# Two sums of weight blocks written over other tiles in a two-layer decoder on one core

## The chip, the core and the metric

The kernel runs on one core of a Trainium2 chip. Its time is the device time of one execution in microseconds (us). The engines are TensorE (PE), VectorE (DVE), ScalarE (ACT), GpSimd (POOL) and SyncE (SP); each runs its own instructions in the order in which they were put on its queue, and waits for the others by semaphores. SP issues the loads of the weights, POOL issues DMAs that add.

## The reference, cut to what matters

```python
def swiglu(h, w_gu, w_down):
    gate, up = jnp.split(h @ w_gu, 2, axis=-1)
    return (jax.nn.silu(gate) * up) @ w_down

def reference(x, mem, ...):
    for l in range(DEPTH):                      # 2 layers, x is 512 tokens x 1024
        x = x + 0.5 * swiglu(rmsnorm(x, g_ffn1[l]), w_ffn1_gu[l], w_ffn1_down[l])
        ...
        x = x + 0.5 * swiglu(rmsnorm(x, g_ffn2[l]), w_ffn2_gu[l], w_ffn2_down[l])
    return rmsnorm(x, g_final)
```

Between the two feed-forward networks (FFNs) of a layer stand a mixer (short convolution beside attention) and a cross-attention; the change does not touch them. All of it is in float32, and the inner width of an FFN is 2816.

## The kernel before, in words

**Precision.** A float32 product is made of three matmuls of a shorter type: each operand is split into a high part (hi) and the rest (lo), and hi times hi, hi times lo and lo times hi are added up. The split of the activations (here called the z split) is a cast on ACT (L644 for the down projection) and a subtraction on DVE (L645).

**Quads.** The FFNs use seven products in place of eight. A quad is four weight blocks 11, 12, 21 and 22; the seven products run in the order 1, 7, 6, 2, 5, 4, 3 (`ORDER`). Their weights are block 11 (product 1), T3 = 22 - 12 (product 7), T2 = T3 + 11 (product 6), block 21 (product 2), T1 = 12 - 11 (product 5), T4 = 21 - T2 (product 4) and block 22 (product 3). The sums T1 to T4 are made by `tt` (L83) on DVE. T3 is made in a tile of its own (`tmp`), T2 is written over T3 in the same tile, T1 over block 11 and T4 over block 21.

**Units.** Each product's weights come in two halves, a and b, called units here; T4a is the sum for the first half. A unit is one tile of 128x1024. `prefetch` splits a unit: the hi is a cast on ACT (L164, `whi<-big`). For the sums (products 7, 6, 5, 4) the lo is a subtraction on DVE (L169). For the raw blocks (products 1, 2, 3; marked "dma") ACT writes the negated hi (L166) and POOL issues a DMA that adds the raw block to it (L167, `wlo<-big`, "adding DMA" below). That DMA reads the raw block until it has landed, so whoever writes over the block waits for it. There are four buffers for units (`UNIT_BUFS`); a unit's hi can be written when PE has released the unit four before it.

**Order of work.** `ffn_plan` lists an FFN's work. An up-projection chunk is a quad of `w_gu` ("product"); a down-projection group is a quad of `w_down` over four or three rows of blocks ("group"). An FFN has three groups: in three of the four FFNs they begin at block 0, 6 and 14, in the last at 2 and 10 (two groups only). In a group the activations of a product are made ready one product ahead (`ready`: sums on DVE at L626, L630, L631, L637; then the z split), and each product is followed by updates of x on DVE (L670). The order on each engine's queue is then set by a scheduler from this program, with the tiles' dependences. Raw blocks come from twelve buffers (`BIG_BUFS`), each filled by a load on SP (L144, 512 KB) as soon as all that read or wrote its last content is done.

Of the kernel before, what the change touches and what calls it, by code (L numbers as in the profile page):

```python
# [8 lines left out]
ALU = mybir.AluOpType  # L9
# [32 lines left out]
class Weights:  # L42
# [30 lines left out]
    def quads(self, w, rows, cols, n):  # L73

        r, tmp = {}, {}
        parts = [(at, min(2, rows[0][1] - at)) for at in range(0, rows[0][1], 2)]

        def raw(q, h):
            at, nk = parts[h]
            r[q, h] = self.raw(w, rows[int(q[0]) - 1][0] + at, nk, (cols[int(q[1]) - 1], n))  # L80

        def tt(out, a, b, op):
            self.nc.vector.tensor_tensor(out=out, in0=a, in1=b, op=op)  # L83
            return out

        def block(q, h):
            return self.tiles[r[q, h]]

        def keep():
            pass  # L90

        def t3(h):
            tmp[h] = self.big((P, parts[h][1], n))
            return tt(tmp[h], block("22", h), block("12", h), ALU.subtract)

        def t2(h):
            return tt(tmp[h], tmp[h], block("11", h), ALU.add)

        def t1(h):
            return tt(block("11", h), block("12", h), block("11", h), ALU.subtract)  # L100

        def t4(h):
            return tt(block("21", h), block("21", h), tmp.pop(h), ALU.subtract)

        def freeing(*qs):
            return lambda: [self.free(r[q]) for q in qs]

        def product(i):
            for h in range(len(parts)):
                if i == 1:  # L110
                    raw("11", h)
                    self.unit(r["11", h], None, keep, "dma")
                elif i == 7:
                    raw("22", h)
                    raw("12", h)
                    self.unit(None, lambda h=h: t3(h), keep)
                elif i == 2:
                    raw("21", h)
                    self.unit(r["21", h], None, keep, "dma")
                elif i == 6:  # L120
                    self.unit(None, lambda h=h: t2(h), keep)
                elif i == 5:
                    self.unit(None, lambda h=h: t1(h), freeing(("11", h), ("12", h)))
                elif i == 4:
                    self.unit(None, lambda h=h: t4(h), freeing(("21", h)))
                else:
                    self.unit(r["22", h], None, freeing(("22", h)), "dma")

        return product
# [1227 lines left out]
```

## Time and profile before

| | us |
|---|---|
| median of 3 runs (2200.09 to 2204.6) | 2200.58 |
| profiled execution, own time | 2204.07 |
| its span in the profile | 2202.3 |
| PE busy in the span | 2134.5 (97%) |
| DVE busy | 1566.2 (71%) |
| ACT busy | 1357.5 (62%) |
| POOL busy | 258.4 (12%) |

The span runs from the first instruction to the last; 1.8 us of the execution's own time lie around it. A line such as `L83 DVE TENSOR_TENSOR big<-big` is an engine's operation at a line of the kernel with what it writes and reads; "idle before, releaser" is the time for which the engine stood idle just ahead of it, and what ended that.

### The profile page before, as it was taken

Reading aid. Unit: us, or ns where it says so; the run is one execution under the profiler, and the core shown is the slowest. Engines: PE = TensorE matmul, PEld = TensorE weight load, DVE = VectorE, ACT = ScalarE, POOL = GpSimd, SP = SyncE. Lnnn points to the kernel's source line nnn. Section 1 sums busy time; section 2 is a strip of 40 time slices with the busy share of each in tenths; the row PEclk is TensorE's granted clock in tenths of the full one; section 3 lists DMA queues with packets and bytes.
Section 4 is the critical chain, followed back from the end, with each engine's and each line's share of the span. In section 5 each row is a group of like instructions: output and inputs, shape, how many; then the busy total and the mean of one; then the engine's idle time right before and its main releaser. Section 6 shows DMA issues by size and latency. Waiting matters only on the chain. (4 is left out here: it accounts for less than half of the span.)

```text
span 2202.3 us, 30504 instructions
## 1 busy us (share of the span) xinstructions
PE 2134.5 (97%) x11602; PEld 1846.0 (84%) x11602; DVE 1566.2 (71%) x2196; ACT 1357.5 (62%) x1990; POOL 258.4 (12%) x293
## 2 busy tenths in 40 slices
PE   9999999999999999999999999999999999989998
PEld 7788889788888888888878888888888888778887
DVE  7677778778754768776777786777786557576775
ACT  7657566566443576667577666656664446556664
POOL 0111110122001011011001111101220010011110
PEclk9999999999999999999999999999999999999999
DMA  6776775223452367677646767642343422677672
GB/s 201 198 171 170 198 168 134 58 77 114 130 140 77 77 161 190 151 183 202 169 109 156 187 171 169 169 108 68 88 126 116 130 87 61 159 172 196 149 182 58
DMA packets 224185, 310.01 MB, mean 141 GB/s; under 512 B 12206, under 2 KB 128166, under 8 KB 224038
## 3 DMA queue, kind: packets, MB, share of 16 engines
q1 hardware_dynamic: 197222, 212.88, 31.7%
q0 software_dynamic: 26784, 95.17, 23.0%
q8 instruction: 91, 1.49, 0.3%
q14 instruction: 56, 0.46, 0.1%
q10 hardware_dynamic: 32, 0.01, 0.0%
HBM read 210.77 MB, written 2.10 MB: 97 GB/s over the span
## 5 line engine op out<-in xcount | busy, mean ns | idle before, releaser
L164 ACT CAST whi<-big 128x1024 fp32r<-128x1024 f32 x582 | 596.8, 1030 | 536.2 <-PE ps L216 227.6
L216 PE MATMUL ps<-whi,t 128*128 128x512 f32 x2624 | 817.1, 390 | 0.4 <-ACT t L220 0.2
L216 PEld LDWEIGHTS ps<-whi,t 128*128 128x128 f32 x2624 | 493.3, 188 | 102.6 <-ACT t L220 0.7
L169 DVE TENSOR_TENSOR wlo<-big,whi 128x1024 fp32r<-128x1024 f32 (+1 forms) x396 | 477.6, 1207 | 90.3 <-ACT whi L164 83.4
L216 PE MATMUL ps<-wlo,t 128*128 128x512 f32 x1312 | 513.3, 391 | 12.5 <-DMA wlo<-big 12.4
L216 PE MATMUL ps<-t,whi 128*128 128x512 f32 x1472 | 456.8, 391 | 1.5 <-ACT whi L855 1.5
L83 DVE TENSOR_TENSOR big<-big 128x1024 f32<-128x1024 f32 x248 | 294.3, 1196 | 219.0 <-DMA wlo<-big 212.6
L658 PE MATMUL ps<-t,whi 128*128 128x256 f32 x2296 | 427.6, 288 | 16.9 <-DVE t L645 15.8
L658 PEld LDWEIGHTS ps<-t,whi 128*128 128x128 f32 x2296 | 366.9, 196 | 21.2 <-DVE t L645 18.3
L658 PE MATMUL ps<-t,wlo 128*128 128x256 f32 x1148 | 330.6, 289 | 19.8 <-DMA wlo<-big 19.7
L216 PEld LDWEIGHTS ps<-t,whi 128*128 128x128 f32 x1472 | 274.5, 188 | 57.2 <-ACT whi L855 2.0
L167 POOL DMA_DIRECT2D wlo<-big x186 | 161.1, 866 | 1280.9 <-ACT wlo L166 732.0
L216 PEld LDWEIGHTS ps<-wlo,t 128*128 128x128 f32 x1312 | 246.7, 188 | 68.3 <-DMA wlo<-big 18.4
L216 PE MATMUL ps<-t,wlo 128*128 128x512 f32 x736 | 286.9, 390 | 1.1 <-DVE wlo L856 1.1
L658 PEld LDWEIGHTS ps<-t,wlo 128*128 128x128 f32 x1148 | 224.6, 196 | 24.2 <-DMA wlo<-big 24.1
L166 ACT ACTIVATE wlo<-big 128x1024 fp32r<-128x1024 f32 (+1 forms) x186 | 193.2, 1039 | 46.1 <-PE ps L216 45.3
L216 PEld LDWEIGHTS ps<-t,wlo 128*128 128x128 f32 x736 | 138.2, 188 | 30.7 <-DVE wlo L856 1.9
L670 DVE SCALAR_TENSOR_TENSOR x<-ps,x 128x512 f32<-128x512 f32 x154 | 102.7, 686 | 18.5 <-PE ps L658 18.3
L552 ACT COPY t<-ps 128x512 f32<-128x512 f32 x120 | 68.5, 586 | 31.2 <-PE ps L216 28.6
L926 POOL TENSOR_TENSOR t<-t,s 128x128 f32<-128x128 f32 (+1 forms) x64 | 60.2, 970 | 216.9 <-DVE s L924 182.3
L645 DVE TENSOR_TENSOR t<-t 128x512 fp32r<-128x512 f32 x88 | 57.0, 651 | 13.7 <-ACT t L644 13.6
L644 ACT CAST t<-t 128x512 fp32r<-128x512 f32 x88 | 50.6, 585 | 25.9 <-DVE t L631 16.4
(185 smaller groups left out, 1988.6 us busy)
## 6 DMA issues: line engine op xcount, KB each, us to landing
wlo<-big POOLq DMA_DIRECT2D x177, 512.0 KB, 5.4
big<-in_w_ffn_gu SPq DMA_DIRECT2D x160, 512.0 KB, 4.4
big<-in_w_ffn_down SPq DMA_DIRECT2D x80, 512.0 KB, 4.4
big<-in_w_mix_in SPq DMA_DIRECT2D x48, 512.0 KB, 3.9
big<-in_w_xkv SPq DMA_DIRECT2D x32, 512.0 KB, 4.0
big<-in_w_ffn_gu SPq DMA_DIRECT2D x32, 256.0 KB, 3.6
big<-in_w_mix_out SPq DMA_DIRECT2D x16, 512.0 KB, 4.6
big<-in_w_xq SPq DMA_DIRECT2D x16, 512.0 KB, 3.7
```

Of the source, the lines that this page charges most:

```text
L83: self.nc.vector.tensor_tensor(out=out, in0=a, in1=b, op=op)
L164: self.nc.scalar.copy(out=hi, in_=src)
L166: self.nc.scalar.activation(out=lo, in_=src, func=AF.Copy, scale=-1.0)
L167: self.nc.gpsimd.dma_start(out=lo, in_=src, accum_op=ALU.add)
L169: self.nc.vector.tensor_tensor(out=lo, in0=src, in1=hi.bitcast(F32), op=ALU.subtract)
L216: mm(ps, x, y, start=first and i == 0, stop=last and i == 2, skip_group_check=chained)
L552: nc.scalar.copy(out=s[i, e], in_=ps)
L644: nc.scalar.copy(out=hi, in_=o)
L645: nc.vector.tensor_tensor(out=lo, in0=o, in1=hi.bitcast(F32), op=ALU.subtract)
L658: mm(bank[f // 2][:, f % 2 * 256 : f % 2 * 256 + 256], w[y][:, k, f * P : (f + 1) * P], z[v][:, k, :], start=i in (1, 7, 2) and p == k == ...
L670: nc.vector.scalar_tensor_tensor(out=o, in0=bank[b].rearrange("p (f t) -> p f t", f=2), scalar=0.5, in1=o, op0=ALU.mult, op1=ALU.add,)
L926: nc.gpsimd.tensor_tensor(out=w[t], in0=w[t], in1=inv[:, t : t + 1].broadcast_to([P, (t + 1) * P]), op=ALU.mult)
```

## The change

```diff
         def t1(h):
-            return tt(block("11", h), block("12", h), block("11", h), ALU.subtract)
+            return tt(block("12", h), block("12", h), block("11", h), ALU.subtract)
 
         def t4(h):
-            return tt(block("21", h), block("21", h), tmp.pop(h), ALU.subtract)
+            return tt(tmp[h], block("21", h), tmp.pop(h), ALU.subtract)
```

T1 is now written over block 12, which no adding DMA reads, and T4 over the tile that holds T2. What the sums hold is the same. The scheduler puts them in other places of DVE's queue.

In the rows below the writes come left of the arrow. The place is the second FFN of layer 0, the group that begins at block 14; big_9360 and big_9381 are its blocks 11 (halves a and b), big_9586 and big_9613 blocks 12, big_9632 and big_9655 blocks 21, big_9771 and big_9793 the tiles of T3, T2 (and now T4). First DVE where the group's T3 is made. Before:

```order
L83 TENSOR_TENSOR big_9771<-big_9584,big_9586 128x1024
L83 TENSOR_TENSOR big_9793<-big_9611,big_9613 128x1024
L561 TENSOR_TENSOR t_9600<-ps_9522,t_9600 128x512
L561 TENSOR_TENSOR t_9602<-ps_9523,t_9602 128x512
L482 SCALAR_TENSOR_TENSOR t_9600<-t_9558,s_7151,t_9600 128x512
L482 SCALAR_TENSOR_TENSOR t_9602<-t_9560,s_7151,t_9602 128x512
L169 TENSOR_TENSOR wlo_9774<-big_9771,whi_9773 128x1024
L482 SCALAR_TENSOR_TENSOR t_9492<-ps_9455,s_7151,t_9492 128x512
```

With the change:

```order
L83 TENSOR_TENSOR big_9771<-big_9584,big_9586 128x1024
L83 TENSOR_TENSOR big_9586<-big_9586,big_9360 128x1024
L83 TENSOR_TENSOR big_9793<-big_9611,big_9613 128x1024
L561 TENSOR_TENSOR t_9600<-ps_9522,t_9600 128x512
L561 TENSOR_TENSOR t_9602<-ps_9523,t_9602 128x512
L83 TENSOR_TENSOR big_9613<-big_9613,big_9381 128x1024
L482 SCALAR_TENSOR_TENSOR t_9600<-t_9558,s_7151,t_9600 128x512
L482 SCALAR_TENSOR_TENSOR t_9602<-t_9560,s_7151,t_9602 128x512
L169 TENSOR_TENSOR wlo_9774<-big_9771,whi_9773 128x1024
```

T1a (`big_9586<-big_9586,big_9360`) stands between T3a and T3b, and T1b (`big_9613<-...`) before the L482; before, both came some ten rows later.

DVE in the same group at product 6, from its first `ready` sum (L630) on; t_9885 and t_9893 are the z splits of product 6, t_9959 and t_9963 those of product 2. Before:

```order
L630 TENSOR_TENSOR t_9881<-r_9501,r_9859 128x512
L83 TENSOR_TENSOR big_9360<-big_9586,big_9360 128x1024
L631 TENSOR_TENSOR t_9880<-t_9881,r_9501 128x512
L83 TENSOR_TENSOR big_9381<-big_9613,big_9381 128x1024
L670 SCALAR_TENSOR_TENSOR x2_156<-ps_9896,x2_156 128x2x256
L645 TENSOR_TENSOR t_9885<-t_9880,t_9884 128x512
L630 TENSOR_TENSOR t_9889<-r_9514,r_9872 128x512
L670 SCALAR_TENSOR_TENSOR x3_157<-ps_9897,x3_157 128x2x256
L631 TENSOR_TENSOR t_9888<-t_9889,r_9514 128x512
L645 TENSOR_TENSOR t_9893<-t_9888,t_9892 128x512
L83 TENSOR_TENSOR big_9632<-big_9632,big_9771 128x1024
L645 TENSOR_TENSOR t_9959<-r_9859,t_9958 128x512
```

With the change:

```order
L630 TENSOR_TENSOR t_9881<-r_9501,r_9859 128x512
L83 TENSOR_TENSOR big_9771<-big_9632,big_9771 128x1024
L631 TENSOR_TENSOR t_9880<-t_9881,r_9501 128x512
L83 TENSOR_TENSOR big_9793<-big_9655,big_9793 128x1024
L670 SCALAR_TENSOR_TENSOR x2_156<-ps_9896,x2_156 128x2x256
L645 TENSOR_TENSOR t_9885<-t_9880,t_9884 128x512
L630 TENSOR_TENSOR t_9889<-r_9514,r_9872 128x512
L670 SCALAR_TENSOR_TENSOR x3_157<-ps_9897,x3_157 128x2x256
L631 TENSOR_TENSOR t_9888<-t_9889,r_9514 128x512
L645 TENSOR_TENSOR t_9893<-t_9888,t_9892 128x512
L645 TENSOR_TENSOR t_9959<-r_9859,t_9958 128x512
```

T4a and T4b stand where T1a and T1b stood, and no L83 stands any more between the z splits of product 6 and of product 2.

DVE at the end of product 5 in the same group; wlo_10120 is the lo of unit 4b. Before:

```order
L670 SCALAR_TENSOR_TENSOR x0_154<-ps_10042,x0_154 128x2x256
L670 SCALAR_TENSOR_TENSOR x1_155<-ps_10043,x1_155 128x2x256
L645 TENSOR_TENSOR t_10111<-r_9859,t_10110 128x512
L83 TENSOR_TENSOR big_9655<-big_9655,big_9793 128x1024
L645 TENSOR_TENSOR t_10115<-r_9872,t_10114 128x512
L637 TENSOR_TENSOR t_10182<-r_9859,t_9880 128x512
L169 TENSOR_TENSOR wlo_10120<-big_9655,whi_10119 128x1024
```

With the change:

```order
L670 SCALAR_TENSOR_TENSOR x0_154<-ps_10042,x0_154 128x2x256
L645 TENSOR_TENSOR t_10111<-r_9859,t_10110 128x512
L670 SCALAR_TENSOR_TENSOR x1_155<-ps_10043,x1_155 128x2x256
L645 TENSOR_TENSOR t_10115<-r_9872,t_10114 128x512
L169 TENSOR_TENSOR wlo_10120<-big_9793,whi_10119 128x1024
```

T4b is gone from here, and the lo of 4b stands ahead of L637.

## Rows read from the trace of the kernel before

**Rows 1.** The page: the line of the quads' sums (busy, mean ns, idle before, releaser).
```profile
L83 DVE TENSOR_TENSOR big<-big 128x1024 f32<-128x1024 f32 x248 | 294.3, 1196 | 219.0 <-DMA wlo<-big 212.6
```

**Rows 2.** The list of waits, engine PE: us in total, times, longest.
```profile
PE ps L658 <- DMA wlo<-big: 19.7, 16, 2.6
PE ps L658 <- DVE t L645: 15.8, 11, 2.3
PE ps L216 <- DMA wlo<-big: 12.4, 13, 3.2
```

**Rows 3.** The list of waits, all engines, same columns: the sums, and ACT behind them.
```profile
DVE big L83 <- DMA wlo<-big: 212.6, 83, 6.7
...
ACT whi L164 <- DVE big L83: 114.4, 40, 5.5
```

**Rows 4.** The timeline of DVE, second FFN, group 14: start, us, engine, line.
```profile
1047.47 1.23 DVE L83 TENSOR_TENSOR big<-big 128x1024 f32<-128x1024 f32 x1 [1.30 <-DMA wlo<-big]
...
1050.09 1.42 DVE L482 SCALAR_TENSOR_TENSOR t<-t,s 128x512 f32<-128x512 f32 x2 [0.20 <-ACT t L479]
...
1061.57 1.22 DVE L83 TENSOR_TENSOR big<-big 128x1024 f32<-128x1024 f32 x1
...
1072.49 1.23 DVE L83 TENSOR_TENSOR big<-big 128x1024 f32<-128x1024 f32 x1 [3.59 <-DMA wlo<-big]
1073.64 0.69 DVE L645 TENSOR_TENSOR t<-r,t 128x512 fp32r<-128x512 f32 x1
```

**Rows 5.** The timeline of POOL, the same group: the adding DMA of block 21.
```profile
1065.30 0.86 POOL L167 DMA_DIRECT2D wlo<-big  x1 [17.84 <-DVE x L670]
```

**Rows 6.** The timeline of PE: matmuls that a z split released, at products 6 and 2.
```profile
939.18 0.38 PE L658 MATMUL ps<-t,whi 128*128 128x256 f32 x1 [1.30 <-DVE t L645]
...
947.19 0.58 PE L658 MATMUL ps<-t,whi 128*128 128x256 f32 x1 [1.92 <-DVE t L645]
...
1065.79 0.39 PE L658 MATMUL ps<-t,whi 128*128 128x256 f32 x1 [1.30 <-DVE t L645]
...
1074.38 0.39 PE L658 MATMUL ps<-t,whi 128*128 128x256 f32 x1 [1.10 <-DVE t L645]
...
2095.78 0.39 PE L658 MATMUL ps<-t,whi 128*128 128x256 f32 x1 [1.29 <-DVE t L645]
...
2103.49 0.38 PE L658 MATMUL ps<-t,whi 128*128 128x256 f32 x1 [1.64 <-DVE t L645]
```

**Rows 7.** The timelines of ACT and POOL, group 14: behind the second T4.
```profile
1083.77 2.00 ACT L164 CAST whi<-big 128x1024 fp32r<-128x1024 f32 x2 [4.32 <-DVE big L83]
...
1087.03 0.86 POOL L167 DMA_DIRECT2D wlo<-big  x1 [18.97 <-ACT wlo L166]
```

**Rows 8.** The timeline of PE: matmuls of product 3 that an adding DMA released.
```profile
239.29 0.39 PE L658 MATMUL ps<-t,wlo 128*128 128x256 f32 x1 [2.36 <-DMA wlo<-big]
...
880.66 0.38 PE L658 MATMUL ps<-t,wlo 128*128 128x256 f32 x1 [2.64 <-DMA wlo<-big]
...
1094.00 0.58 PE L658 MATMUL ps<-t,wlo 128*128 128x256 f32 x1 [1.97 <-DMA wlo<-big]
```

**Rows 9.** The timelines of SP, POOL and PE: the first product chunk of layer 1.
```profile
1139.20 0.37 SPq L144 DMA_DIRECT2D big<-in_w_ffn_gu  x1
...
1139.97 0.86 POOL L167 DMA_DIRECT2D wlo<-big  x1 [2.26 <-ACT wlo L166]
...
1147.91 0.50 PE L216 MATMUL ps<-wlo,t 128*128 128x512 f32 x1 [3.21 <-DMA wlo<-big]
```

**Rows 10.** Four stretches: PE, PEld, DVE, ACT, POOL busy, PEclk, DMA share, GB/s.
```profile
155.30:158.70 3.40, 3.40 (x18) 3.40 (x18) 1.22 (x1) 1.04 (x1) 0.00 (x0) 0.50 1.07 206
1066.70:1070.10 3.40, 3.40 (x18) 3.40 (x17) 1.52 (x3) 1.34 (x3) 0.86 (x1) 0.50 1.00 245
1238.50:1241.90 3.40, 3.40 (x29) 3.40 (x30) 2.42 (x3) 0.89 (x1) 0.86 (x1) 1.00 1.06 193
1978.00:1981.40 3.40, 3.40 (x19) 3.40 (x18) 3.40 (x6) 0.00 (x0) 0.00 (x0) 0.50 0.84 249
```

## The prediction

> **What bounds the kernel now.** PE is busy for 2134.5 us of a span of 2202.3 (the table above), so what a reordering can win lies in the 68 us in which PE stands idle, and in the stretches in which its clock is halved. I read the list of waits first, then the timelines around the places it names. DVE's sums wait 212.6 us for adding DMAs, 83 times [rows 3], which is nearly all the idle time in front of L83 [rows 1], and ACT's casts of units wait 114.4 us for those sums [rows 3]. That is a lot, and little of it reaches PE: PE waits 15.8 us for z splits, 19.7 us for adding DMAs in the groups and 12.4 us for them in the product chunks [rows 2]. 47.9 us is the ceiling; the sum below goes by these, not by the 212.6.
>
> How the two meet is seen in one group. T4a overwrites block 21, so it waits 3.59 us for the adding DMA that reads block 21 and was issued at 1065.30 [rows 4, 5]. The z split of product 2 (the L645 at 1073.64) stands behind it on DVE though it needs nothing of it, and PE idles 1.10 us until 1074.38 [rows 4, 6]. Ten us on, T4b is late in DVE's queue; the casts of units 4b and 3a on ACT wait 4.32 us for it, the adding DMA of 3a is issued at 1087.03 only, and PE stands for 1.97 us [rows 7, 8].
>
> **Part A: T4a no longer waits for an adding DMA.** The order shows T4a and T4b ahead of the z splits of product 6 and none behind. Of the 11 waits for a z split, five are at product 6 (first 939.18, last 2095.78, about 1.3 us each, 6.4 in all) and six at product 2 (first 947.19, last 2103.49), so these six hold 15.8 - 6.4 = 9.4 us [rows 2, 6]. What is late next is the landing itself: T4a could start at 1072.49 because the DMA had landed, and PE had come to product 2 at 1074.38 - 1.10 = 1073.28, 0.8 us later [rows 4, 6]. In the first group shown PE came at 945.27 [rows 6], about when T4a was released there. I take 0.4 us off for such places: **-9.0 us**; bounds -9.4 and 0 (the landing just takes the place of the split).
>
> **Part B: T1 moves ahead of product 6.** T1a now stands between T3a and T3b, where DVE waits 1.30 us for an adding DMA: it costs nothing, and if that wait were gone it would cost what T1b costs. T1b stands behind that wait, in front of L482, where the only cover is an idle 0.20 us [rows 4]. An L83 moves the next row back by 1.15 us (1072.49 to 1073.64), so everything behind it comes 0.95 us later, as T4a and T4b just fill the places that T1a and T1b held. Behind it stands the z split of product 6, for which PE waits in five groups already: 5 x 0.95 = 4.8 us. In a sixth (the first FFN's group at 6) one update of x comes ahead of that split as well, 1.15 + 0.6 us less what room there is; I take 1.5. In the other five groups T1b falls in idle time of DVE or ahead of work with room. **+6.3 us**; bounds 0 (the wait of T3 ends later or earlier than before and swallows it) and +8.
>
> **Part C: T4b is early, so 4b and 3a are cast on time.** Of the 16 waits for an adding DMA in groups, seven (first and largest 2.36 at 239.29, then 1.97 at 1094.00 among them) come of a late T4b: 7.4 us; two more, 1.2 us, are just behind the last group, among the 13 of the product chunks [rows 2, 8]. ACT's double cast at 1083.77 would go as soon as PE gives the buffers back; that is 1.6 us earlier for 3a, by my reading of where PE releases unit 5a, so of 1.97 us about 0.4 stay. Over all: **-7.6 us**. In the three first groups of an FFN (6.8 us, the largest 2.64 at 880.66 [rows 8]) I count nothing: the cast of 3a gains 0.5 us only before it meets its buffer's release, and two matmuls of the next chunk that filled that wait no longer stand in it. Bounds: 0 and -12.
>
> **Part D: loads go earlier.** Block 11 comes free when T2 has read it rather than when T1 is split. In the first chunk of layer 1, loads start at 1139.20, together with the adding DMA of unit 2b issued at 1139.97, which lands only just ahead of 1147.91 (7.9 us) and costs PE 3.21 us [rows 9]. With T2 releasing them the first two loads start some 8 us earlier, and are through when that DMA starts. Such first chunks hold 8.5 of the 12.4 us [rows 2]. I take 2.5 of the 3.21, 1.9 in the first chunk of the first FFN and 1.3 in the last FFN: **-5.7 us**; bounds 0 and -8.5.
>
> There the trace shows a slow adding DMA beside loads, and no more. The Trainium skill (DMA: Bandwidth & Descriptors, Queues, rings and completion order) says that each DMA engine goes round the queues that have work, packet by packet: loads and adding DMAs then share whatever time they overlap, and moving loads only moves the sharing. The trace agrees in so far as 7.9 us stand beside loads; by that rule part D is worth 0 if the loads meet another adding DMA, and the sum would be -14.5 in place of -20.2.
>
> **Clock.** Eight stretches of 3.4 us run at a granted clock of 0.50, the 1.2 GHz level (first 155.30, last 1978.00), each just behind gaps of PE; each loses 1.7 us. But a gap of 1.87 us ahead of 1238.50 was followed by a clock of 1.00, while product 6's gap of 1.30 was followed by 0.50 at 1066.70 [rows 6, 10]: the length of one gap does not decide. Five of the eight follow gaps that A, C and D take away. Product 6's longer gaps (2.2 us) may bring new ones; I take half of the places, 2.5. Net 2.5 x 1.7: **-4.2 us**; bounds -8.5 and +3.4.
>
> In the product chunks T4's waits of some 5 us cost PE nothing now, as the units there are made 2 to 5 us ahead, and I cost their end at nothing too; without that room each would show as a wait of PE at L216.
>
> **Sum:** -9.0 + 6.3 - 7.6 - 5.7 - 4.2 = -20.2 us against the profiled execution's own 2204.1 (its span and 1.8 us around it): 2183.9. That execution is 3.5 us above the median of the three runs, 2200.58; against the median the sum would be 2180.4. The profiled one may hold a halved stretch or two more than a usual run, so I stay near the upper: **2184**.
>
> **Rivals.** (1) **Product 6 becomes the bound and carries its delay on: slower.** T1b delays L644 and the ACT work behind it, so the adding DMA of 2a is issued later as well. If it takes over 0.8 us longer than PE is held up, the room between 1072.49 and 1073.28 is gone, its landing takes the place of T4a's wait and A is worth nothing. All six gaps at product 6 then halve the clock (6 - 4 stretches, +3.4), C and D give 2 each: 6.3 + 3.4 - 4 = +5.7, **2210**. For it: DVE has no idle time behind L482 there but 0.20 us. Against: PE is held up by the same 0.95, so the room stays. (2) **The clock falls at all the longer gaps** while the rest goes as forecast: -16 + 1.7 = -14, **2190**. For it 1066.70, against it 1238.50. (3) **The loads only meet other adding DMAs** and D is nothing: **2190**. For it, the 7.9 us beside loads; against it, in the order the loads wait for a landed DMA of block 11 or 21. (4) **Landings replace half of it**: A 4.5, C 2.5, D 2.5, clock nothing: -9.5 + 6.3 = -3.2, **2201**, no change. For it: 0.8 us is little room, and 3a's DMA took nearly 7 us (1087.03 to 1094.00). (5) **The change does not do what it says**: T4 would meet a new wait for the readers of T2's tile. The cast and the split of product 6 both stand ahead of it and are done by then, so this gets little; 2204.
>
> **Chances.** Forecast 0.55, (1) 0.06, (2) 0.17, (3) 0.10, (4) 0.10, (5) 0.02. What a measurement of this kernel can tell from no change is about 0.2%, 4.4 us. Faster: forecast, (2) and (3), 0.82. Same: (4) and (5), 0.12. Slower: (1), 0.06. The range starts where B is hidden by T3's wait and no new stretch is halved (-20.2 - 6.3 - 4.3 = -30.8, 2173; a little lower for the median) and ends at (4): 2172 to 2200.
>
> **What would show it.** In the profile after: DVE's waits at L83 for adding DMAs fall from 83 to about the 36 that belong to T3, some 90 us; PE's waits for z splits fall to five or six, each near 2.2 us, all at product 6, and none at product 2; the group of 19.7 falls to about 12; in the first chunk of layer 1 the adding DMA of 2b lands in under 6 us. Wrong would be a wait of PE for `wlo<-big` at product 2 as long as the split's was (rival 1 or 4), a wait of T4 for anything, or gaps at product 6 no longer than 1.3 us (B mis-sized).

## The result, and the profile after

The changed kernel takes 2174.94 us (median of 4, 2173.55 to 2176.87) against 2202.59 for the kernel before on the same chip (2200.09 to 2206.55): a ratio of 0.9873, 95% interval 0.9854 to 0.9892, 28 us faster. The profiled executions lie at 2176.87 and 2204.07, 27.2 us apart, and the accounts below go by these two.

The page of the changed kernel, to be held against the PE line of the table of before and [rows 1]:

```profile
PE 2124.5 (98%) x11602; PEld 1840.2 (85%) x11602; DVE 1568.4 (72%) x2196; ACT 1359.4 (62%) x1990; POOL 258.9 (12%) x293
...
L83 DVE TENSOR_TENSOR big<-big 128x1024 f32<-128x1024 f32 x248 | 294.0, 1196 | 61.1 <-DMA wlo<-big 58.0
```

The span is now 2175.1 us. PE stands idle for 50.6 us of it where it was 67.8, which is 17.2 us less. PE's busy time fell by 10.0 us with the same matmuls. DVE's idle time ahead of L83 fell from 219.0 to 61.1 us, and DVE is as busy as it was: the work stayed, and most of the waiting moved. DVE's idle time as a whole fell by 29 us only (from 636.1 to 606.7), since DVE now waits longer for ACT's casts ahead of the lo of a unit (L169). The list of waits for all engines, against [rows 3] (us in total, times, longest):

```profile
ACT whi L164 <- DVE big L83: 62.2, 20, 4.6
DVE big L83 <- DMA wlo<-big: 58.0, 29, 3.6
...
DVE wlo L169 <- ACT whi L164: 218.0, 190, 6.5
```

Before, the last of these was:

```profile
DVE wlo L169 <- ACT whi L164: 83.4, 130, 4.4
```

The waits of PE, the same columns, against [rows 2]:

```profile
PE ps L658 <- DMA wlo<-big: 11.5, 8, 2.6
PE ps L216 <- DMA wlo<-big: 10.2, 11, 2.1
PE ps L658 <- DVE t L645: 7.8, 6, 1.3
...
PE ps L658 <- ACT t L644: 2.2, 4, 0.9
```

Waits of PE for adding DMAs in the groups went from 19.7 to 11.5 us, those in the chunks from 12.4 to 10.2, those for z splits from 15.8 to 7.8; waits for a z cast (L644) rose from 0.7 to 2.2. These six at L645 are all at product 6; at product 2 there is none left.

DVE in the second FFN's group at 14, the group of [rows 4] (start, us, engine, line):

```profile
1042.89 3.74 DVE L83 TENSOR_TENSOR big<-big 128x1024 f32<-128x1024 f32 x3 [3.63 <-DMA wlo<-big]
...
1047.75 1.22 DVE L83 TENSOR_TENSOR big<-big 128x1024 f32<-128x1024 f32 x1
...
1060.13 1.22 DVE L83 TENSOR_TENSOR big<-big 128x1024 f32<-128x1024 f32 x1
...
1061.87 1.22 DVE L83 TENSOR_TENSOR big<-big 128x1024 f32<-128x1024 f32 x1
...
1063.60 0.69 DVE L645 TENSOR_TENSOR t<-t 128x512 fp32r<-128x512 f32 x1
...
1067.38 0.68 DVE L645 TENSOR_TENSOR t<-r,t 128x512 fp32r<-128x512 f32 x1
```

The first row holds T3a, T1a and T3b without a pause, where 1.30 us of waiting stood ahead of T3b. T1b (1047.75) follows, T4a and T4b (1060.13 and 1061.87) wait for nothing, and the z split of product 2 (1067.38) comes straight behind those of product 6. In [rows 4] it came at 1073.64.

PE at product 6, against [rows 6]; the first row is a group that had no gap before:

```profile
215.87 0.39 PE L658 MATMUL ps<-t,whi 128*128 128x256 f32 x1 [1.30 <-DVE t L645]
...
940.54 0.58 PE L658 MATMUL ps<-t,whi 128*128 128x256 f32 x1 [1.30 <-DVE t L645]
...
1062.66 0.39 PE L658 MATMUL ps<-t,whi 128*128 128x256 f32 x1 [0.53 <-ACT t L644]
...
1064.34 0.39 PE L658 MATMUL ps<-t,whi 128*128 128x256 f32 x1 [1.30 <-DVE t L645]
```

The wait for the low part (L645) is 1.30 us as it was; what grows is the wait for the cast ahead of it (0.53 here, where it was 0.30).

The first product chunk of layer 1, the rows of [rows 9]: POOL issues the adding DMA of unit 2b, PE's first matmul with it follows.

```profile
1132.40 0.86 POOL L167 DMA_DIRECT2D wlo<-big  x1 [2.26 <-ACT wlo L166]
...
1137.77 0.50 PE L216 MATMUL ps<-wlo,t 128*128 128x512 f32 x1 [0.90 <-DMA wlo<-big]
```

5.4 us from issue to use where it was 7.9, and a wait of 0.90 us where it was 3.21. The two loads that started 0.8 us ahead of this DMA and 1.0 us behind it now start 8.6 and 6.5 us ahead of it; two others start 1.5 and 2.9 us behind it. But the first chunk of layer 0's second FFN, which had no gap, now has one (POOL, SP, PE):

```profile
784.57 0.85 POOL L167 DMA_DIRECT2D wlo<-big  x1 [3.52 <-ACT wlo L166]
...
784.85 2.16 SPq L144 DMA_DIRECT2D big<-in_w_ffn_gu  x2
...
792.05 0.50 PE L216 MATMUL ps<-wlo,t 128*128 128x512 f32 x1 [2.13 <-DMA wlo<-big]
```

Here two loads start 0.3 and 2.1 us behind the adding DMA of 2b, which takes 7.4 us. In the kernel before, the same two started 1.9 and 3.0 us behind it, and it took 4.9 us. The list of DMA queues (packets, MB, share of the 16 DMA engines) shows what it waits for. From 785.5 to 788.0 only the loads' queue moves bytes:

```profile
q1 hardware_dynamic: 157, 0.32, 78.5%
```

The bytes of the adding DMA follow when the first load is through. In the first chunk of layer 1 it is the other way round: from 1132.4 to 1136.7 only POOL's queue moves bytes, though two loads are issued in that time. So in these places the transfers take turns as wholes, and what counts is whether a load goes out ahead of the adding DMA or just behind it.

The granted clock (columns as in [rows 10]): four stretches at 0.50 (first 155.40, last 2070.30) where there were eight; behind the gap of 1064.34 there is none.

```profile
155.40:158.80 3.40, 3.40 (x18) 3.40 (x18) 2.73 (x3) 0.88 (x1) 0.00 (x0) 0.50 1.03 195
216.90:220.30 3.40, 3.40 (x18) 3.40 (x17) 2.01 (x4) 1.34 (x4) 0.87 (x1) 0.50 1.05 198
940.50:943.90 3.40, 3.36 (x15) 3.36 (x16) 2.72 (x5) 2.29 (x4) 1.29 (x2) 0.50 0.81 153
1064.40:1067.80 3.40, 3.40 (x28) 3.40 (x29) 2.71 (x5) 2.72 (x5) 1.18 (x2) 1.00 0.82 154
2070.30:2073.70 3.40, 3.40 (x19) 3.40 (x18) 2.31 (x4) 1.53 (x3) 0.86 (x1) 0.50 0.99 187
```

### The profile page after: what moved, and what is told of

Read it like the earlier page. It is cut to its first block, busy times and chain, and to the rows that moved or that the text cites. A ratio compares the mean times of both kernels' runs of the same rounds, so it can differ in the third digit from the quotient of the medians.

```text
span 2175.1 us, 30582 instructions
## 1 busy us (share of the span) xinstructions
PE 2124.5 (98%) x11602; PEld 1840.2 (85%) x11602; DVE 1568.4 (72%) x2196; ACT 1359.4 (62%) x1990; POOL 258.9 (12%) x293
## 5 line engine op out<-in xcount | busy, mean ns | idle before, releaser
L169 DVE TENSOR_TENSOR wlo<-big,whi 128x1024 fp32r<-128x1024 f32 (+1 forms) x396 | 478.1, 1207 | 222.1 <-ACT whi L164 218.0
L216 PE MATMUL ps<-wlo,t 128*128 128x512 f32 x1312 | 512.4, 391 | 10.5 <-DMA wlo<-big 10.2
L658 PE MATMUL ps<-t,wlo 128*128 128x256 f32 x1148 | 327.6, 286 | 11.5 <-DMA wlo<-big 11.5
L83 DVE TENSOR_TENSOR big<-big 128x1024 f32<-128x1024 f32 x248 | 294.0, 1196 | 61.1 <-DMA wlo<-big 58.0
L926 POOL TENSOR_TENSOR t<-t,s 128x128 f32<-128x128 f32 (+1 forms) x64 | 60.2, 970 | 216.9 <-DVE s L924 182.2
L645 DVE TENSOR_TENSOR t<-t 128x512 fp32r<-128x512 f32 x88 | 57.0, 650 | 15.4 <-ACT t L644 15.1
L644 ACT CAST t<-t 128x512 fp32r<-128x512 f32 x88 | 51.1, 584 | 23.3 <-DVE t L631 15.3
```

Of the source, the lines that this page charges most:

```text
L169: self.nc.vector.tensor_tensor(out=lo, in0=src, in1=hi.bitcast(F32), op=ALU.subtract)
L216: mm(ps, x, y, start=first and i == 0, stop=last and i == 2, skip_group_check=chained)
L644: nc.scalar.copy(out=hi, in_=o)
L645: nc.vector.tensor_tensor(out=lo, in0=o, in1=hi.bitcast(F32), op=ALU.subtract)
L658: mm(bank[f // 2][:, f % 2 * 256 : f % 2 * 256 + 256], w[y][:, k, f * P : (f + 1) * P], z[v][:, k, :], start=i in (1, 7, 2) and p == k == ...
L926: nc.gpsimd.tensor_tensor(out=w[t], in0=w[t], in1=inv[:, t : t + 1].broadcast_to([P, (t + 1) * P]), op=ALU.mult)
```

## The experiments

All were timed beside the kernel before on the same chip. In the text, "product 6" stands for the waits of PE for z splits and casts there.

**Each half of the change alone.** T4 over T2's tile alone, then T1 over block 12 alone:

```diff
-            return tt(block("21", h), block("21", h), tmp.pop(h), ALU.subtract)
+            return tt(tmp[h], block("21", h), tmp.pop(h), ALU.subtract)
```
```diff
-            return tt(block("11", h), block("12", h), block("11", h), ALU.subtract)
+            return tt(block("12", h), block("12", h), block("11", h), ALU.subtract)
```

> Only T4 goes over T2's tile; T1 stays on block 11. Theory: T4's wait for an adding DMA, with the z splits and casts behind it, is the cost, so the six waits of PE for z splits at product 2 (9.4 us) and the seven for product 3 (7.4 us) go, with some half-clock stretches (4 to 8 us); but in DVE's order T1a, T1b and T4a now all stand ahead of the first z split of product 6, 1.15 us more than before, so the gaps at product 6 grow by 5 x 1.15 + 1.5 = 7 us. About 2188 beside 2202.6 for the kernel before, slower than the full change. Rival (T1's move brings the gain): within 4 us of the kernel before, waits at product 2 still there.

> Only T1 goes over block 12; T4 stays on block 21 and still waits for the adding DMA. Theory: what counts is what stands behind T4's wait. In the order both z splits of product 2 now stand ahead of T4a, so the six waits at product 2 (9.4 us) go without T4 having lost its wait (DVE keeps about 47 waits of T4); T1a and T1b no longer stand between L630 and the z split of product 6, whose gaps shrink from 1.3 to 1.5 us to under 1; T4b stays late, so the seven waits at product 3 (7.4 us) stay. About 2185. Rival (T4's wait itself has to go): no more than 4 us faster than the kernel before.

T4 alone: 2180.38 us, ratio 0.9907 (0.9891 to 0.9924). T1 alone: 2186.64, ratio 0.9923 (0.9905 to 0.9941). PE's waits with T4 alone:

```profile
PE ps L216 <- DMA wlo<-big: 12.9, 11, 2.1
PE ps L658 <- DVE t L645: 12.4, 10, 1.8
PE ps L658 <- DMA wlo<-big: 11.3, 8, 2.4
```

The six gaps at product 2 and the seven at product 3 are gone, as expected; the ten waits for z splits are all at product 6, 12.4 us where the full change has 7.8 and 2.2. So with T1 late three sums stand ahead of the first split there and T4b ahead of the second, and moving T1 out of that place is worth something by itself. The forecast of this run (2188) was 8 us too slow: the gaps at product 6 were sized about right (they grew by 5.4 us in all, to 12.4, where 7 had been expected), and what gave more is PE's busy time, 11.2 us less, with a mean granted clock of 0.996 where it was 0.993.

T1 alone: waits of DVE, then of PE.

```profile
DVE big L83 <- DMA wlo<-big: 189.1, 74, 6.0
```

```profile
PE ps L658 <- DMA wlo<-big: 23.2, 17, 2.6
```

DVE waits 189 us for adding DMAs where it was 212.6, and PE's waits for z splits fall to 1.0 us (three of 0.3, all at product 6), since in this order the splits of product 2 stand ahead of T4a. So what costs is what stands behind a wait; the wait of T4 by itself costs little. The waits at product 3 that were expected to stay fell as well, from 7.4 to 2.3 us. But the adding DMAs in the groups cost 23.2 us, more than before. One of them (POOL, then PE):

```profile
1067.64 0.86 POOL L167 DMA_DIRECT2D wlo<-big  x1 [2.89 <-ACT wlo L166]
...
1073.64 0.39 PE L658 MATMUL ps<-t,wlo 128*128 128x256 f32 x1 [2.06 <-DMA wlo<-big]
```

This is unit 2b. PE comes to product 2 earlier because product 6 holds it up no longer, and the DMA also goes out later: in this order three casts of activations (L644) stand on ACT just ahead of 2b's negated hi, and POOL issues at 1067.64 what it issues at 1065.75 in the changed kernel. That is the first rival's "landing takes the place of the split", without longer gaps at product 6; in the six groups it costs 8.6 us here. That the time forecast for this run (2185) came out is luck in part: these 8.6 us were not in it, and some 5 us of the waits at product 3 went that were to stay.

**What stands ahead of product 6's split.** The sums u + v of both halves are issued ahead of the differences:

```diff
+            for p, nk in pairs(c) if i == 6 else ():
+                u, v = (rows[(c, e), p][:, :nk, 256:] for e in "uv")
+                sums[c, 5, p] = T(shape=(P, 2, 256))[:, :nk, :]
+                nc.vector.tensor_add(out=sums[c, 5, p], in0=u, in1=v)
             for p, nk in pairs(c):
...
                     elif i == 6:
-                        v = rows[(c, "v"), p][:, :nk, :]
-                        sums[c, 5, p] = T(shape=(P, 2, 256))[:, :nk, :]
-                        nc.vector.tensor_add(out=sums[c, 5, p], in0=u[:, :, 256:], in1=v[:, :, 256:])
```

> The changed kernel again, on the chip of the three runs that follow: about 2175, with waits for z splits at product 6 of some 10 us.

> The changed kernel, and at product 6 of a group the sums u + v of both halves come first and the differences behind them, so that in DVE's order only one T4 and no update of x stands ahead of the first z split of product 6. Theory (what stands ahead of that split sets the gaps at product 6): the split comes 1.15 us earlier, and the 10 us at product 6 fall to 4 to 6; about 2170. Rival (the gaps at product 6 only cover late landings of product 2's adding DMAs): the waits for z splits fall as much and the waits for adding DMAs in the groups grow by as much; 2175.

The change again took 2173.27 us (ratio 0.9864, 0.9843 to 0.9885), the version with the sums first 2167.89 (0.9840, 0.9819 to 0.9861). Waits of PE, first the change again, then the sums first (its lines 645 and 658 are 646 and 659):

```profile
PE ps L216 <- DMA wlo<-big: 11.0, 13, 2.1
PE ps L658 <- DMA wlo<-big: 9.1, 8, 1.6
PE ps L658 <- DVE t L645: 7.8, 6, 1.3
...
PE ps L658 <- ACT t L644: 1.7, 3, 0.8
```

```profile
PE ps L216 <- DMA wlo<-big: 11.2, 13, 2.2
PE ps L659 <- DMA wlo<-big: 11.2, 11, 2.3
PE ps L659 <- DVE t L646: 2.8, 5, 0.7
```

Product 6 falls from 9.5 to 2.8 us. The adding DMAs in the groups grow by 2.1; new waits at product 2 hold 1.1 us. So the theory holds, with a small share for the rival: of 6.7 us won at one place some 2 come back at the next, and the median moved by 5.4. The intervals of this pair overlap (0.9843 to 0.9885 and 0.9819 to 0.9861); the same step is seen once more, and larger, in the last pair of runs below.

**Unit 2b of the first chunks.** Its lo is made on DVE in place of the adding DMA:

```diff
-                    self.unit(r["21", h], None, keep, "dma")
+                    self.unit(r["21", h], None, keep, False if first and h else "dma")
```

(`first` is true for the quads of chunk 1.)

> The changed kernel, and in the first product chunk of each FFN the lo of unit 2b is made by a subtraction on DVE and not by an adding DMA (four units). Theory: the 6.1 us that PE waits there for that DMA in the changed kernel (2.05, 2.13, 0.90, 1.04) come of its sharing the DMA engines with loads that were freed earlier, and they go, with a half-clock stretch or two: 2166 to 2170 beside about 2175 for the changed kernel. Rival (the unit is late for another reason, its casts or its buffer): PE waits there as long for DVE's lo, and the time stays at 2175.

> The change with the first chunks' unit 2b split on DVE, again, on one chip with the run that follows. With the sums first it was worth 8.6 us (2167.9 to 2159.3), on the change alone 1.3 at most. If the first measurement held a bad draw of landings, 2165 to 2168 now; if the gain needs the gaps at product 6 gone (their half-clock stretches and the later adding DMAs take it back), 2172 to 2175 again, with five or so half-clock stretches.

2173.69 us (ratio 0.9878, 0.9859 to 0.9896) and again 2172.25 (0.9844, 0.9816 to 0.9871). The two ratios lie on either side of the change's own (0.9873 and 0.9864), so by itself this is worth something between nothing and the 5 us that were expected, and the runs don't settle it. The gaps themselves did go. PE's waits in the second of these runs:

```profile
PE ps L658 <- DVE t L645: 7.8, 6, 1.3
PE ps L216 <- DMA wlo<-big: 5.8, 8, 2.3
```

In the chunks 5.8 us stay of 10.2 to 11.0 (8.2 in the first of the two, where later units wait more); at unit 2b of the first chunks no wait is left in either. That much of the theory holds: without that adding DMA there is no gap. The granted clock, 0.996 and 0.997 in the changed kernel's two profiles, was 0.996 and 0.995 in these, so no halved stretch went with the gaps; product 6's gaps are still there (7.8 us at L645).

**A pool of its own for T3.** T3 waits because its tile is the buffer that block 22 has just left. Given two buffers of its own (the pool of activations gives up four of 47), it waits for no adding DMA:

```diff
-T_BUFS = 47
+T_BUFS = 43
...
-            tmp[h] = self.big((P, parts[h][1], n))
+            tmp[h] = self.tmp_pool.tile(
+                [P, parts[h][1], n], F32, name="tmp", tag="tmp", padded_shape=[P, 1024 // n, n]
+            )
...
+    tmp_pool = ctx.enter_context(tc.tile_pool(name="tmp", bufs=2))
```

> The changed kernel, and T3 gets a pool of its own with two buffers in place of one of the twelve that hold blocks (the pool of activations gives up four of 47), so T3 no longer waits for the adding DMA of the chunk before. Theory (T3's wait at the head of a group makes product 6's split late, T1b only lengthens it): the 29 waits of 58 us at L83 go, and so do the 10 us at product 6; 2163 to 2168. Rival (T1 and T4 ahead of the split are the cause): the waits at product 6 stay at 6 us or more; 2173 or more. A third (two loads more run ahead, beside adding DMAs): waits for adding DMAs grow by what the splits give.

> The two runs before together: no gap at product 6 is left. If landings do not take their place, 2160 to 2166; if product 2's adding DMAs do (as with T1 alone moved), 2170 to 2175.

2205.48 us (ratio 1.0018, 1.0003 to 1.0032), and with the sums first as well 2203.49 (1.0004, 0.9992 to 1.0015): all that the change had won is lost. T3's waits for adding DMAs are gone and so is every wait at product 6, as the theory said; but the adding DMAs cost 52.5 us in place of 21.7 (lines 219 and 661 are 216 and 658 of the kernel before):

```profile
PE ps L219 <- DMA wlo<-big: 34.9, 31, 3.5
PE ps L661 <- DMA wlo<-big: 17.6, 18, 2.7
```

Some 40 us of it are at product 1, in chunks and groups, where the changed kernel waits 5.9 us. The waits account for some 21 us of the 29 between the two profiles (30.8 more at adding DMAs, 10.0 less at product 6); PE is also busy for 8.2 us more at the same mean clock, 0.996, and why is open. Two readings were left: two more blocks loaded ahead, or the loads' new places in time. The next run takes the two blocks away again:

```diff
-BIG_BUFS = 12
+BIG_BUFS = 10
...
-                W.limit = BIG_BUFS - 4
+                W.limit = BIG_BUFS - 2
...
-            W.limit = BIG_BUFS - 2
+            W.limit = BIG_BUFS
```

(on top of the first of these two runs, so without the sums first, and with `T_BUFS` at 47).

> As the run with a pool of two for T3, but blocks have ten buffers in place of twelve, so no load goes further ahead than in the changed kernel (and activations have their 47 again). Theory (in the run before, two more loads at a time ran beside product 1's adding DMAs, which landed after 7.5 to 9.4 us where 5 is usual): the waits of PE at product 1, 35 us there, fall below 10, T3 still waits for nothing and product 6 has no gap: 2162 to 2168. Rival (T3's wait kept DVE and ACT from other work that now comes ahead of product 1's): the waits at product 1 stay, 2195 to 2205.

2203.68 us (ratio 1.0006, 0.9991 to 1.0021): my theory of the two extra blocks fell, and so did the shortage of activations as a cause. What is left is when the loads go out, not how many are ahead. SP, POOL and PE in this run, at the second chunk of the first FFN:

```profile
74.52 3.56 SPq L146 DMA_DIRECT2D big<-in_w_ffn_down  x2
...
75.38 0.87 POOL L169 DMA_DIRECT2D wlo<-big  x1 [1.84 <-ACT wlo L168]
78.09 0.87 POOL L169 DMA_DIRECT2D wlo<-big  x1 [1.85 <-ACT wlo L168]
...
86.53 0.50 PE L219 MATMUL ps<-wlo,t 128*128 128x512 f32 x1 [1.06 <-DMA wlo<-big]
```

The row of SP holds two loads, the second of them at 77.74. They go out as soon as block 22's buffers are free, and beside them stand the two adding DMAs of product 1 (75.38 and 78.09), the second of which is used 8.4 us after its issue. In the changed kernel T3 takes these two buffers, no load goes out between 70.25 and 87.67, and the same two DMAs (issued at 77.16 and 79.88) land in 5.3 and 6.0 us. So T3's hold on these buffers, with the wait that looked like pure loss on DVE, keeps loads off product 1's DMAs. It is so all over the kernel: of the 186 adding DMAs, 10 in the changed kernel have a load that was issued less than 1 us ahead or 0.5 us behind, and 48 in this run; these land after 7.6 and 8.0 us on average, the others after 5.1 and 5.0.

The rival on record for this run, other work on DVE and ACT ahead of product 1's, had 2195 to 2205, where the time fell, but the rows speak against it. The adding DMAs that PE waits for here are issued as far ahead of PE as in the changed kernel (6.5 us on average, 6.3 there); they land 1.9 us later (7.6 and 5.7). A run that holds back these loads alone was not made.

**The two that helped, together.** Sums first, and the first chunks' 2b on DVE:

> Sums first at product 6, and the first chunks' unit 2b split on DVE, on top of the change: the two gains lie in different places (groups and first chunks), so if they add up 2164 to 2167; if what the first chunks give is taken back by later adding DMAs, as it was without the sums first, 2167 to 2169.

> The fastest version again (sums first, first chunks' 2b on DVE): 2158 to 2161, at most two half-clock stretches.

2159.33 us (ratio 0.9802, 0.9778 to 0.9825), and again 2161.52 (0.9795, 0.9775 to 0.9814): faster than both kernels, and by 5 us more than the first forecast, for which the two gains just add up. PE's waits in the first of them:

```profile
PE ps L659 <- DMA wlo<-big: 10.8, 9, 2.3
PE ps L216 <- DMA wlo<-big: 6.3, 8, 1.6
PE ps L659 <- DVE t L646: 3.2, 5, 0.7
```

The mean granted clock is 0.999 and 0.998. On one chip the second of them stands 10.7 us below the change with 2b alone (2172.25): some 6 us are product 6's gaps (10.4 to 4.1 in the two profiles), and (0.998 - 0.995) x 2160 = 6.5 us the clock: one stretch at 0.50 in place of five. But the clock's share is not product 6's alone. Of the four that are gone, two stood behind product 6's gaps (at 936.8 and 2063.2) and two behind landings of adding DMAs (875.3 and 2100.7, behind waits of 1.83 and 2.32 us). Why a given gap is followed by a halved stretch and another is not, stays open.

## Why the prediction was right, and where its sizes were off

The forecast was 2184 with a range of 2172 to 2200, and faster with 0.82; measured 2174.94. The sum was -20.2 us against the profiled execution; it came to -27.2. The direction and the mechanism held: T4 no longer waits, the splits and casts behind it are in time, and gaps and stretches at half clock go. That the number came within 10 us is luck in part: B's cost was set 3.3 us too high and D's gain 4.1 us too large, the clock's gain 2.6 us too small, and 5 us were in no term. By steps:

- **Part A (-9.0): right, with help that was not in it.** All six gaps at product 2 are gone, 9.4 us. The feared landing behind them did not show, for two reasons. PE is held up at product 6: with T4 alone the adding DMA of 2a takes 6.0 to 6.8 us in these six groups and still lands 1.2 to 2.3 us ahead of PE. And with T1 moved that DMA is faster: it took 5.0 to 7.2 us before (6.3 or more in five of the six) and takes 4.5 to 4.8 now, as the loads into block 11's buffers go out earlier; with T4 alone they do not. In the group at 14, before (issue of 2a at 1065.30, [rows 5]) and after:

```profile
1062.82 2.62 SPq L144 DMA_DIRECT2D big<-in_w_ffn_gu  x4
```
```profile
1055.09 2.24 SPq L144 DMA_DIRECT2D big<-in_w_ffn_gu  x4
...
1063.86 0.86 POOL L167 DMA_DIRECT2D wlo<-big  x1 [18.08 <-DVE x L670]
```

  This is part D's mechanism at work in the groups, where I had not counted it. With T1 alone and with the sums first, where product 6 hardly holds PE up, 2a lands 0.04 to 0.6 us ahead of PE in the same groups, and at 2b landings cost 8.6 us with T1 alone.
- **Part B (+6.3): right in sign, half as large.** Product 6 went from 7.0 us (6.4 at L645 and 0.6 at the casts) to 10.0, which is +3.0: 1.6 in the sixth group and 1.4 in the five others, where 4.8 was taken. The step that failed is "everything behind it comes 0.95 us later". In the group shown T1b does add that, but T3a and T3b came some 0.4 to 0.6 us earlier against PE, because product 3's adding DMAs landed a little sooner, and the 1.30 us wait ahead of T3b went into T1a. The bound "T3's wait ends earlier and swallows it" was named, but not weighed. The sixth group (215.87) did get its gap: 1.6 where 1.5 was taken. Among the signs of being wrong stood "gaps at product 6 no longer than 1.3 us (B mis-sized)": two of the six are at 1.3, the others, with the wait for the cast, at 1.6 to 2.2.
- **Part C (-7.6): right.** The seven gaps at product 3 in the groups are gone (7.4 us). The two behind the last group did not go (1.2 before, 1.8 after), and the first groups of the FFNs kept theirs (6.8 before, 5.9 and 4.2 in two profiles), as counted.
- **Part D (-5.7): a third of it.** The "first chunks" of the prediction's 8.5 us take in two waits in the second chunk of the last FFN (2.2 us); by the same count there are 6.9 us now. Layer 1's first chunk gave the 2.5 us that I took, and the last FFN the 1.3, though at that second chunk (2.2 to 0.3; its first chunk grew from 0.5 to 1.0). The first FFN's chunk gave nothing (its loads still start beside the adding DMAs), and the second FFN of layer 0 got a new gap of 2.1 us: T4 over T2's tile frees block 21 as soon as its DMA has landed, and that load now goes out 0.3 us behind the next adding DMA (784.57 to 792.05). That is the third rival, in part. The Trainium skill (DMA: Bandwidth & Descriptors, Queues, rings and completion order) says that the engines go round the queues packet by packet. The trace agrees that the queues take turns: from 785.5 to 788.0 only the loads' moves bytes, from 1132.4 to 1136.7 only POOL's. What the prediction drew from the rule, that an adding DMA and a load share whatever time they overlap, does not show in these places: one waits for the other. Beside two loads the adding DMA took 7.4 us where the first went out 0.3 us behind it, and 5.3 and 4.9 where they went out 1.5 us behind it or later. The runs with T3's own pool show it most plainly, with 48 such meetings in place of 10 and a kernel 30 us slower. Where I summed a gain from earlier loads, I should have looked up which adding DMA each meets next.
- **Clock (-4.2): too small.** Four stretches at 0.50 against eight, 6.8 us. The new ones behind product 6 came about as counted, three (216.9, 940.5, 2070.3) for 2.5. What failed is that the stretches left standing would stay: of the three not in the way of A, C and D, those at 1066.70 and 1414.8 went too. Each profile is one draw: the second one of the changed kernel has three such stretches, and single executions of the kernel before have mean clocks from 0.990 to 0.996.
- A, B, C, D and clock as measured come to -9.4 + 3.0 - 7.4 - 1.6 - 6.8 = -22.2. Of the 5 us that are left, 1.8 are spread over PE's other waits (17.2 us of idle time less 15.4), and 3.2 are busy time of PE beyond the halved stretches (10.0 less 6.8), which I cannot place.

Of the rivals, the second (clock at every longer gap) and the fourth (landings replace half) are out by the numbers above; the fifth by the rows of T4a and T4b, which wait for nothing. The first did not come about: in the six groups the DMA of 2a lands 1.5 to 3.4 us ahead of PE.

## What to carry to other kernels

Look not at how long an engine waits but at what stands behind the waiting instruction and who needs that: 155 us of DVE's waits for DMAs went, and PE's idle time fell by 17; with T1 alone moved most of DVE's waits stayed, and PE's waits for splits still fell from 15.8 to 1.0. A sum that is written over a tile which no DMA reads is free to move, and the scheduler will move it ahead of something else; read the new order for what it now holds up. Before a wait is taken away at the head of a chain, see which transfers it has been holding back.

## What was not expected

Two loads beside an adding DMA of 512 KB can cost it 3 us or next to nothing. It took 5.3 us with no load beside it (77.16), 5.3 and 4.9 with loads issued 1.5 us behind it or later, and 6.3 to 8.4 in the places named here where one was issued from 0.9 us ahead of it to 0.3 us behind it. Units are made so closely ahead of PE that these 3 us decide: giving T3 its own buffers removed 58 us of DVE's waits and all of product 6's gaps, and made the kernel 30 us slower than the change. That a longer wait on one engine can be what keeps two transfers apart was in none of the theories.
